# Moving the semaphore reset at the end of a kernel beside its last store

One NeuronCore of one Trainium2 chip runs the kernel. The metric is the device time of one execution in microseconds. The kernel before takes 121.06 us in its first three runs (median).

Some terms. The engines are PE (TensorE), ACT (ScalarE), DVE (VectorE), GpSimd (POOL in the views) and SP (SyncE), which here issues the transfers. A semaphore is a counter that instructions and transfers change and for whose value an engine can wait; each of the big transfers here adds sixteen to its semaphore when it lands, in steps of one. An event-semaphore instruction only waits for and changes semaphores. A drain is another instruction that can carry such waits and changes; the reset drain also names a range of semaphores. A range clear sets a range of semaphores to zero. A barrier is a place in the program that all engines must reach before any goes on.

## The reference

```python
# x, y: (1024, 4096) float32
z = x + y
out = 0.5 * z * (1 + np.tanh(np.sqrt(2 / np.pi) * (z + 0.044715 * z ** 3)))
```

The kernel reads 33.55 MB, writes 16.78 MB and does a few operations per element in between.

## The kernel before

Inputs come in by eight loads of 4 MB, the result goes out by three stores of 8, 5 and 3 MB, all on SP's queue. Eight semaphores count the completions of these eleven transfers; the last store shares its semaphore, number 103, with an early load, so that 32 means that both have landed. Cuts from the kernel, with "..." where lines are left out and two comments added:

```python
    stores = [16384, 10240, 6144]            # columns of float32, 128 partitions
    ...
    def store(i):
        a, b = sr[i]
        ins = nc.sync.dma_start(out=ov[:, a:b], in_=zt[:, a:b])
    ...
    ctx.close()
    tc.close()
    tc.compile()
    begin_early(nc, 2)                       # the first two loads start before the opening barrier
    wait_late(nc)
```

The framework ends a program so: SP waits for everything, all engines meet in a barrier, GpSimd resets and clears the semaphores 99 to 109, all engines meet again. An earlier tuning step had already split this. SP waits for everything but the last store; the barriers run while that store is under way; GpSimd's reset drain, which carries the wait for the last store, and its range clear stand at the very end:

```python
def wait_late(nc):
    body, end = nc.main_func.blocks[1:3]
    SP, POOL = mybir.EngineType.SP, mybir.EngineType.Pool
    last = [i for i in body.instructions if isinstance(i, mybir.InstDMACopy)][-1]
    (sem,) = [u.id for u in last.sync_info.on_update]
    all_done = end.instructions[0]
    clear = next(i for i in end.instructions if isinstance(i, mybir.InstDrain) and i.is_reset_sema)
    assert all_done.engine == SP and clear.engine == POOL and clear.sync_info is None
    waits = all_done.sync_info.on_wait
    its = [w for w in waits if w.id == sem]
    assert len(its) == 1
    rest = [w for w in waits if w.id != sem]

    def drain(old, waits, **reset):
        return mybir.InstDrain(
            name=old.name, engine=old.engine, debug=old.debug,
            sync_info=mybir.SyncInfo(on_wait=waits, on_update=[]), **reset
        )

    at = end.instructions.index(clear)
    clears = [
        drain(
            clear, its, is_reset_sema=True,
            reset_range_start=clear.reset_range_start, reset_range_stop=clear.reset_range_stop,
        ),
        end.instructions[at + 1],
    ]
    assert isinstance(clears[1], mybir.InstISA) and clears[1].engine == POOL
    del end.instructions[at : at + 2]
    end.instructions[0] = drain(all_done, rest, is_reset_sema=False)
    end.instructions.extend(clears)
```

On GpSimd, the end of the program is then, in order:

```
drain                                            first barrier
event semaphore: wait for 4 arrivals, subtract 4
event semaphore: release the 4 others
drain                                            second barrier
event semaphore: wait for 4 arrivals, subtract 4
event semaphore: release the 4 others
drain with reset of 99..109, waits for semaphore 103 >= 32
range clear of 99..109
```

## Time and profile before

| | before |
|---|---|
| time, first three runs | 121.06, 121.23, 121.06 us |
| span of the profiled run, first to last instruction | 118.914 us |
| last store issued | 106.771 us |
| last data packet of it ends | 118.254 us |
| its 16 semaphore increments | 118.329 to 118.689 us |
| reset drain | 118.713 to 118.790 us |
| range clear | 118.819 to 118.914 us |
| GpSimd's step of the runtime's closing barrier | 119.441 us |
| last step of the closing barrier | 120.870 us |

The instants come from the trace's records of instructions, packets and semaphore changes, counted from the start of the span. (The prediction gives 118.259 for the last data packet; that is the end of the last of the 4-byte packets that follow the data and count. Nothing hangs on it.) After the program's last instruction the runtime adds a closing part. In it, semaphore 2 takes nine steps (the first barrier, its last step at 119.726), then some 250 semaphores are written, then it takes nine steps more (120.514 to 120.870); both barriers together are called the closing barrier here. The **tail** is the distance from the sixteenth increment of the last store to the last step of the closing barrier: here 120.870 − 118.689 = 2.181 us. The **own part** is the distance from the same increment to the waiting engine's own step of that barrier: here 119.441 − 118.689 = 0.752 us.

The list of DMA issues on the page gives the last store, with its size and the time from issue to landing:

```profile
out_dram<-z SPq DMA_DIRECT2D x1, 3072.0 KB, 11.9
```

The reader is to see that 11.9 us of store separate its issue from the end.

### The profile page before, as it was taken

The numbers are of one execution on the slowest core, as the hardware profiler recorded it, in microseconds if no ns is written. First come the engines' busy times: TensorE is split into PE (matmuls) and PEld (weight loads), VectorE is DVE, ScalarE is ACT, GpSimd is POOL, SyncE is SP. The second block draws the span as 40 slices with busy tenths as digits, with TensorE's granted clock in tenths as the row PEclk, the third lists the DMA queues.
The fourth block names the chain that finished last, engine by engine and source line by source line (L and its number), as shares of the span: only waits on it lengthen the run. The fifth ranks groups of instructions, "written<-read, shape, count | busy, mean of one in ns | idle before, by whom it ended". The sixth has DMA issues, their size and how long they took to land.

```text
span 118.9 us, 170 instructions
## 1 busy us (share of the span) xinstructions
DVE 73.7 (62%) x35; ACT 61.0 (51%) x34; POOL 69.7 (59%) x19
## 2 busy tenths in 40 slices
DVE  0000000635799995749999958999994999990000
ACT  4000000064888865197698657888829769800000
POOL 0000000699995199999959999959999990000000
DMA  7989898989999898989899998998898889999996
GB/s 254 452 364 518 353 529 353 518 364 474 408 430 452 364 518 353 529 353 518 364 474 408 408 474 353 529 529 353 353 683 375 353 353 441 441 441 441 397 397 265
DMA packets 1584, 50.33 MB, mean 423 GB/s; under 512 B 176, under 2 KB 176, under 8 KB 176
## 3 DMA queue, kind: packets, MB, share of 16 engines
q1 hardware_dynamic: 1584, 50.33, 98.6%
HBM read 33.55 MB, written 16.78 MB: 423 GB/s over the span
## 4 chain that ended last, share of the span: by engine, by line
DMA 51%; POOL 26%; POOLq 4%; DVE 4%; DVEq 2%; ACT 2%; issue 0%; SPq 0%
DMA y<-in_y_dram 51%; POOL z L145 26%; POOLq L223 4%; DVE w L156 2%; DVEq L223 2%; DVE z L168 2%; ACT w L150 2%; SPq L121 0%; POOLq L145 0%
## 5 line engine op out<-in xcount | busy, mean ns | idle before, releaser
L145 POOL TENSOR_TENSOR z<-z,y 128x2048 f32<-128x2048 f32 x15 | 69.4, 4661 | 28.2 <-DMA y<-in_y_dram 28.2
L150 ACT ACTIVATE w<-z 128x2048 f32<-128x2048 f32 x16 | 30.1, 1882 | 37.6 <-DVE z L145 21.4
L156 DVE SCALAR_TENSOR_TENSOR w<-w,z 128x2048 f32<-128x2048 f32 x16 | 36.7, 2295 | 11.2 <-ACT w L150 11.0
L168 DVE TENSOR_TENSOR z<-w,z 128x2048 f32<-128x2048 f32 (+1 forms) x17 | 35.9, 2155 | 0.0
L161 ACT ACTIVATE w<-w 128x2048 f32<-128x2048 f32 x16 | 29.7, 1855 | 4.4 <-DVE w L156 4.3
L145 DVE TENSOR_TENSOR z<-z,y 128x2048 f32<-128x2048 f32 x1 | 2.3, 2292 | 20.4 <-DMA y<-in_y_dram 20.4
L208 ACT ACT_TABLE_LOAD x1 | 1.3, 1283 | 1.3 <-PEq L240 1.3
L207 DVE MEMSET one<- 128x1 f32 x1 | 0.1, 59 | 1.3 <-PEq L240 1.3
L240 POOL MEMSET const-float32-0.0<- 128x1 f32 x1 | 0.1, 99 | 0.2 <-issue 0.2
L208 ACT ACTIVATE one<-one 128x1 f32<-128x1 f32 x1 | 0.2, 203 | 0.0
L240 POOL MEMSET const-bfloat16-1.0<- 128x1 bf16 x1 | 0.1, 101 | 0.0
L240 POOL MEMSET const-uint8-127<- 128x1 uint8 x1 | 0.1, 101 | 0.0
L240 POOL MEMSET const-float32-1.0<- 128x1 f32 x1 | 0.1, 98 | 0.0
## 6 DMA issues: line engine op xcount, KB each, us to landing
z<-in_x_dram SPq DMA_DIRECT2D x4, 4096.0 KB, 31.3
y<-in_y_dram SPq DMA_DIRECT2D x4, 4096.0 KB, 22.2
out_dram<-z SPq DMA_DIRECT2D x1, 5120.0 KB, 15.8
out_dram<-z SPq DMA_DIRECT2D x1, 3072.0 KB, 11.9
out_dram<-z SPq DMA_DIRECT2D x1, 22.0
```

Source lines behind the costliest of these rows:

```text
L145: eng.tensor_add(out=zt[:, a:b], in0=zt[:, a:b], in1=yt[s][:, o : o + b - a])
L150: nc.scalar.activation(out=wt[c], in_=zt[:, a:b], func=act.Square, scale=root)
L156: nc.vector.scalar_tensor_tensor(out=wt[c], in0=wt[c], scalar=c1, in1=zt[:, a:b], op0=alu.add, op1=alu.mult)
L161: nc.scalar.activation(out=wt[c], in_=wt[c], func=act.Sigmoid)
L168: ins = nc.vector.tensor_mul(out=zt[:, a + o : a + o + n], in0=wt[c][:, o : o + n], in1=zt[:, a + o : a + o + n],)
L207: nc.vector.memset(one, 0.0)
L208: nc.scalar.activation(out=one, in_=one, func=act.Sigmoid)
L223: tc.compile()
L240: nc = _bacc.Bacc("TRN2", target_bir_lowering=False, num_devices=1)
```

## The change

The intent is to leave nothing after the landing but a wait. GpSimd resets and clears beside the running store. It must leave out the last store's semaphore, which is still counting, so the range is cleared in two parts around it. At the end an event-semaphore instruction waits for the count and takes it back to zero by subtraction.

```diff
--- before.py
+++ after.py
@@ -26,36 +26,44 @@
 def wait_late(nc):
 
 
-    body, end = nc.main_func.blocks[1:3]
-    SP, POOL = mybir.EngineType.SP, mybir.EngineType.Pool
-    last = [i for i in body.instructions if isinstance(i, mybir.InstDMACopy)][-1]
+
+    body, end = (b.instructions for b in nc.main_func.blocks[1:3])
+    last = [i for i in body if isinstance(i, mybir.InstDMACopy)][-1]
     (sem,) = [u.id for u in last.sync_info.on_update]
-    all_done = end.instructions[0]
-    clear = next(i for i in end.instructions if isinstance(i, mybir.InstDrain) and i.is_reset_sema)
-    assert all_done.engine == SP and clear.engine == POOL and clear.sync_info is None
+    all_done = end[0]
+    reset = next(i for i in end if isinstance(i, mybir.InstDrain) and i.is_reset_sema)
+    at = end.index(reset)
+    clear = end[at + 1]
+    first, stop = reset.reset_range_start, reset.reset_range_stop
+    assert all_done.engine == mybir.EngineType.SP and reset.engine == mybir.EngineType.Pool
+    assert isinstance(clear, mybir.InstISA) and clear.engine == mybir.EngineType.Pool
     waits = all_done.sync_info.on_wait
-    its = [w for w in waits if w.id == sem]
-    assert len(its) == 1
-    rest = [w for w in waits if w.id != sem]
-
-    def drain(old, waits, **reset):
-        return mybir.InstDrain(
-            name=old.name, engine=old.engine, debug=old.debug,
-            sync_info=mybir.SyncInfo(on_wait=waits, on_update=[]), **reset
+    (its,) = [w for w in waits if w.id == sem]
+
+    end[0] = mybir.InstDrain(
+        name=all_done.name, engine=all_done.engine, debug=all_done.debug, is_reset_sema=False,
+        sync_info=mybir.SyncInfo(on_wait=[w for w in waits if w.id != sem], on_update=[]),
+    )
+    parts = []
+    for f, e in ((first, sem), (sem + 1, stop)):
+        if f < e:
+            nc.gpsimd.sem_clear(range(f, e))
+            parts.append(nc.cur_bb.bb.instructions.pop())
+    end[at + 1 : at + 2] = parts
+    end.append(
+        mybir.InstEventSemaphore(
+            name=clear.name, engine=clear.engine, debug=clear.debug,
+            sync_info=mybir.SyncInfo(
+                on_wait=[its],
+                on_update=[
+                    mybir.SyncUpdate(
+                        sync_type="semaphore", id=sem, ant_name=its.ant_name,
+                        update_mode="sem-sub-imm", update_value=its.wait_value,
+                    )
+                ],
+            ),
         )
-
-    at = end.instructions.index(clear)
-    clears = [
-        drain(
-            clear, its, is_reset_sema=True,
-            reset_range_start=clear.reset_range_start, reset_range_stop=clear.reset_range_stop,
-        ),
-        end.instructions[at + 1],
-    ]
-    assert isinstance(clears[1], mybir.InstISA) and clears[1].engine == POOL
-    del end.instructions[at : at + 2]
-    end.instructions[0] = drain(all_done, rest, is_reset_sema=False)
-    end.instructions.extend(clears)
+    )
 
 
 @with_exitstack
```

On GpSimd the end is now:

```
drain, event semaphore, event semaphore          first barrier
drain with reset of 99..109
range clear of 99..102
range clear of 104..109
drain, event semaphore, event semaphore          second barrier
event semaphore: wait for semaphore 103 >= 32, subtract 32
```

## The prediction

> **What bounds the kernel now.** I read the page from the top: span, busy shares, the row of slices, the DMA queue. After that I looked only at the end, because the change touches nothing else.
>
> ```profile
> span 118.9 us, 170 instructions
> DVE 73.7 (62%) x35; ACT 61.0 (51%) x34; POOL 69.7 (59%) x19
> DMA  7989898989999898989899998998898889999996
> q1 hardware_dynamic: 1584, 50.33, 98.6%
> ```
>
> No compute engine is above 62%, while the packets of the one DMA queue fill 98.6% of the span. The kernel is bound by moving 50.33 MB, and the diff leaves every load, add, activation and store as it is. So the first 106 us cannot move by design. Next I listed the DMA queue's own waits and cut the last twelve microseconds into windows.
>
> ```profile
> SPq L223 <- DMA out_dram<-z: 4.2, 1, 4.2
> ...
> 106.70:111.40 4.70, 0.04 (x1) 0.00 (x0) 0.00 (x0) 1.00 0.84 363
> 111.40:118.20 6.80, 0.00 (x0) 0.00 (x0) 0.00 (x0) 1.00 0.94 405
> 118.20:118.72 0.52, 0.00 (x0) 0.00 (x0) 0.00 (x0) 1.00 0.00 0
> 118.72:118.91 0.19, 0.00 (x0) 0.00 (x0) 0.00 (x0) 1.00 0.00 0
> ```
>
> The reader is to see four stages. SP waits 4.2 us for the second store. Until 118.2 the last store moves at about 400 GB/s with no engine at work. For 0.5 us no byte moves, because the store's completion is still on its way. In the last 0.19 us nothing moves and nothing is waited for. Which instructions fill that last piece is told by the line on which the program's end is recorded, first in the window 118 to 119, then in the window 111 to 113:
>
> ```profile
> L223 POOLq DRAIN  x1: 77/77/77, 118.7 to 118.7; - x1
> L223 POOLq EVENT_SEMAPHORE_RANGE_CLEAR  x1: 95/95/95, 118.8 to 118.8; - x1
> ...
> L223 POOLq EVENT_SEMAPHORE  x4: 17/17/17, 111.7 to 112.1; - x4
> L223 POOLq DRAIN  x1: 41/41/41, 111.9 to 111.9; - x1
> ```
>
> The first two lines are the last two instructions of the span: the reset drain, 77 ns, and the range clear, 95 ns. The next two say that GpSimd (POOL) was through the closing barriers at about 112.1 and then sat in the drain's wait for 6.6 us. The chain of waits is of no use here: it counts working instructions and stops with a drain on DVE that began at 104.5, long before the end.
>
> The trace's own records give these instants more finely (from the span's start): the last data packets of the last store end at 118.259; its sixteen semaphore increments are recorded from 118.329 to 118.689; the drain starts at 118.713 and ends at 118.790; the range clear runs from 118.819 to 118.914, where the span ends. The clears of semaphores 99 to 109 are recorded at 118.840 to 118.887.
>
> **What the Trainium skill says.** "Perfetto Trace Analysis", section "Per-instruction lifecycle", sequencer-only instruction: the reported start is the moment when all semaphores are satisfied, and the wait is outside the reported window. The trace agrees: the drain's record begins 24 ns after the sixteenth increment and not at 112. "DMA: Bandwidth & Descriptors", section "Why a DMA increments its semaphore by 16 and not by 1": each engine that took part posts one increment after its own data, and only the full count means that everything landed. The trace agrees, with sixteen records spread over 360 ns; so the wait cannot be taken earlier, it can only be followed by less. "Runtime: NRT & Kernel Launch", section "The ~15µs preamble/postamble breakdown": after the kernel a barrier waits for all engines, then each engine resets 51 semaphores, then another barrier. The trace agrees in kind: the barrier semaphore, number 2, has two steps at 112.45 and 112.49, then none until 119.44, which is 0.53 us after GpSimd's last instruction; resets of 51 semaphores each follow, and the last barrier step is at 120.87.
>
> **The change part by part.**
>
> 1. Removed from the end, between the arrival of the last increment and the end of the span: the drain (77 ns), the gap after it (118.819 − 118.790 = 29 ns) and the range clear (95 ns). Sum 77 + 29 + 95 = 201 ns. All of it is on the path: GpSimd is the only engine still running, and nothing else works in the last window.
>
> 2. Added at the end: one event-semaphore instruction that waits for the last store's count and subtracts it. The same kind is in the barriers on the same engine at 17 ns each (the row x4 above; one of these also waits and subtracts). In the second barrier the last increment is recorded at 112.012, the instruction starts at 112.037, 25 ns later, and its subtraction is recorded at 112.062. So the reaction, 24 ns for the drain and 25 ns for this kind, is the same, and the duration is 17 ns instead of 201.
>
> 3. Moved to the middle: the reset drain and now two clears, one below and one above the last store's semaphore, between the first and the second barrier. Cost there: the drain 77, a gap 29, a clear 95, a gap 29, a clear 95, together 325 ns on GpSimd, holding the second barrier and the other engines up by about as much: its end goes from about 112.2 to about 112.5. The last count comes at 118.689, so 6.2 us of slack stay. Nothing of it is on the path. The two clears write semaphores, no bytes of the store's; I give the DMA nothing for them.
>
> 4. The sum: the span ends at 118.689 + 0.024 + 0.017 = 118.730 instead of 118.914, which is 0.184 us less. The time around the span, 121.08 − 118.91 = 2.17 us in the profiled run, has a closing part that starts only when GpSimd arrives (the barrier semaphore stood still for 7 us), so I carry the saving over one to one: 121.06 − 0.18 = 120.88 us, or 0.15%.
>
> **The rivals.**
>
> First: the saving is hidden, because something else ends then. For it: a tail of 2.17 us lies outside the span and I see only its semaphores. Against: all other engines are through their last instruction by 112.22, and the barrier's third step comes only after GpSimd. If it were so, the time would stay 121.06.
>
> Second: the saving is larger. GpSimd needs 0.53 us from its last instruction to its step of the closing barrier; the first step, at 112.45, comes 0.24 us after the last engine to leave the barrier before it has ended. If part of the surplus of 0.29 us is GpSimd settling after the drain and the clear, it could go too, and the time would be about 120.6 to 120.75. Nothing in the trace says what the 0.53 us are, so I count this only as a longer lower tail.
>
> Third: the new wait costs what the old pair cost. If the subtraction had to be confirmed before the engine goes on, the gain would shrink by some tens of nanoseconds, to 120.93 or so. Against: the same kind in the barrier is 17 ns and its subtraction is recorded 25 ns after its start, within the time that the range clear takes for its own writes (21 to 68 ns after its start).
>
> Fourth: the reset drain, now run while the store is under way and still naming the whole range, wipes the half-full count of the last store's semaphore. The wait would then never be met and the kernel would hang. Against: in the trace of before no semaphore changes during the drain (118.713 to 118.790); the first zeroing is recorded at 118.840, inside the range clear. The drain as such clears nothing that is recorded.
>
> Fifth: the stores run differently by chance. The three runs before span 0.17 us, as much as the expected gain; one slow arrival can hide it in a single run, though hardly in medians of several.
>
> **Range and chances.** Central value 120.88. The lower end, 120.70, is the central value less about 0.18 for the second rival and for scatter; the upper end, 121.05, is the central value and the 0.17 us by which the runs of before differ, which is also nearly no gain at all. Over 2% faster would be below 118.64, a saving of 2.4 us, twelve times what the removed instructions last: 0.005. Over 2% slower would need a new wait of 2.4 us at the end: 0.005. Within 2%: 0.99.
>
> **What would show each step.** In the changed profile the window of the end should hold one event semaphore of about 17 ns on GpSimd in place of the drain and the range clear, starting some 25 ns after the sixteenth increment. Two range clears and a drain of about 77 ns should stand near 112, and the second barrier should be about 0.3 us later there. The distance from the last increment to the span's end should be about 0.04 us instead of 0.225; it is the cleanest number, because it does not contain the store's own scatter. The distance from there to the last barrier step should stay 1.96 us; if it shrinks, the second rival is right; if it grows by 0.18, the first. The prediction fails if the time stays within some hundredths of 121.06 in paired runs although the end is shorter, or if the last store itself lands at another time.

## The result

| | before | changed |
|---|---|---|
| time, median of six runs | 121.09 us (121.03 to 121.23) | 120.94 us (120.86 to 120.96) |
| ratio | | 0.9985, interval 0.9972 to 0.9998 |
| span of the profiled run | 118.914 us | 118.683 us |
| last store issued | 106.771 us | 106.776 us |
| sixteenth increment | 118.689 us | 118.641 us |
| last instruction starts, ends | 118.819, 118.914 us | 118.666, 118.683 us |
| increment to end of span | 0.225 us | 0.042 us |
| own part | 0.752 us | 0.603 us |
| tail | 2.181 us | 2.036 us |

Ratios and intervals are worked out from runs of the same rounds; they are not quite the ratios of the medians quoted. The gain is 0.15%, by the interval between 0.02 and 0.34 us. The page of the changed kernel:

```profile
span 118.7 us, 172 instructions
DMA  7989898989989898989999898998899889999896
q1 hardware_dynamic: 1584, 50.33, 98.8%
```

Same packets, same bytes, the same fill of the queue; two instructions more. The windows of the end in the changed kernel (stretch, its length, busy time of DVE, ACT and POOL with counts, clock, DMA share, GB/s):

```profile
111.40:118.20 6.80, 0.00 (x0) 0.00 (x0) 0.00 (x0) 1.00 0.93 401
118.20:118.67 0.47, 0.00 (x0) 0.00 (x0) 0.00 (x0) 1.00 0.00 0
118.67:118.68 0.01, 0.00 (x0) 0.00 (x0) 0.00 (x0) 1.00 0.00 0
```

The piece after the landing, 0.19 us before, has shrunk to one of 0.01 (two instructions' records to one). The line on which the program's end is recorded is now L231. Its instructions in the window 118 to 119 of the changed kernel (count, shortest, median and longest in ns, first and last start):

```profile
L231 POOLq EVENT_SEMAPHORE  x1: 17/17/17, 118.7 to 118.7; - x1
```

The same line in the window 111 to 113:

```profile
L231 POOLq EVENT_SEMAPHORE  x4: 17/17/17, 111.7 to 112.3; - x4
L231 POOLq DRAIN  x2: 34/58/82, 111.8 to 112.1; - x2
```

And the line of the two clears:

```profile
L50 POOLq EVENT_SEMAPHORE_RANGE_CLEAR  x2: 53/60/66, 112.0 to 112.0; - x2
```

All as the diff says: one event semaphore of 17 ns at the end, both clears and a second drain near 112 us. The drain and the clear that lasted 77 and 95 ns are gone from the end. And yet the tail is not 183 ns shorter, as the span's end is (0.225 − 0.042), but 145 (2.181 − 2.036). The 38 ns between are the one thing to be explained.

**What the measured time contains.** In the trace of before the time of the same execution, 121.08, exceeds the last barrier step, 120.870, by 0.21 us. In the changed kernel it is 120.89 − 120.677 = 0.21. In the twelve traces below it is 0.22 to 0.23 in eleven; the exception is told there. So, where all else is equal, a nanosecond of tail is a nanosecond of time. This matters for the method: the time scatters by tenths of a microsecond, the tail by one to three nanoseconds in the two kernels that were traced twice (the kernel before has one trace).

### The profile page after: what moved, and what is told of

It reads as the page before. It is cut to its first block, busy times and chain, and to the rows that moved or that the text cites. A ratio compares the mean times of both kernels' runs of the same rounds, so it can differ in the third digit from the quotient of the medians.

```text
span 118.7 us, 172 instructions
## 1 busy us (share of the span) xinstructions
DVE 73.7 (62%) x35; ACT 61.0 (51%) x34; POOL 69.6 (59%) x19
## 4 chain that ended last, share of the span: by engine, by line
DMA 51%; POOL 26%; POOLq 4%; DVE 4%; DVEq 2%; ACT 2%; issue 0%; SPq 0%
DMA y<-in_y_dram 51%; POOL z L153 26%; POOLq L231 4%; DVE w L164 2%; DVEq L231 2%; DVE z L176 2%; ACT w L158 2%; SPq L129 0%; POOLq L153 0%
```

## The experiments

Two theories of the 38 ns. **The record**: an instruction at the end costs its recorded duration, and the 38 ns are something else in the runtime's closing part. **The slot**: an instruction costs the time from its start to the next one's start, and part of that lies outside the record. The barrier in the middle of the trace of before shows slots on GpSimd: event semaphore with subtraction 112.037 to 112.115, 78 ns, though recorded as 17; drain at the end 118.713 to 118.819, 106 ns, recorded as 77. A third question is what the remaining half microsecond of GpSimd's own part is. Every run gave the right result. All edits are to `wait_late` of the changed kernel and are shown shortened; `late(name, engine, waits, updates, kind)` builds one instruction with the given waits and semaphore updates, an event semaphore by default. `its` is the wait for 32, `sub` the subtraction of 32; `at_least(n)` and `subtract(n)` stand for the same with another number.

### Eight more instructions at the end, first try

```diff
+    for k in range(8):
+        end.append(late(f"I-9000{k}", POOL, [its], []))
     end.append(late("", POOL, [its], [sub]))
```

> Eight more event-semaphore instructions on GpSimd, each waiting on the last store's count that is already met, stand ahead of the changed kernel's last one. They magnify one disputed number: what such an instruction costs at the end. Theory of the record: it costs its recorded 17 ns, so 8 x 17 = 0.14 us over the changed kernel: about 121.08 us, and the distance from the sixteenth increment of the last store to the last step of the closing barrier (call it the tail; 2.181 us in the kernel before, 2.036 in the changed one) becomes 2.17. Theory of the slot: it costs what lies between the starts of two neighbours on GpSimd, 78 to 79 ns in the barrier of the trace before, so 8 x 78 = 0.62 us: about 121.56 us, tail 2.66. Rival that time at the end is hidden outside the span: the tail may grow, but the time stays 120.94.

Measured: tail 2.390 us; time 121.35 us, ratio to before 1.0022 (1.0008 to 1.0037). The window 118.2 to 121 of this kernel shows why neither number fits:

```profile
L232 POOLq EVENT_SEMAPHORE  x5: 17/43/43, 119.4 to 119.7; - x5
```

Five, not nine: the compiler had packed the waits in pairs (43 ns with two waits, 17 with one). These are four instructions more than in the changed kernel, and they made the tail 2.390 − 2.036 = 0.354 us longer, 88 ns for each on average. As a test of the two theories this run is spoilt. It still answers the first rival: the tail is 0.209 us above that of before, and the time is 0.0022 x 121.1 = 0.27 us above it (0.10 to 0.45). What happens at the end is not hidden.

### Eight more instructions, mended

```diff
+    for k in range(8):     # wait for 32, 31, ... 25, subtract 1 each
+        end.append(late(f"I-9000{k}", POOL, [at_least(32 - k)], [subtract(1)]))
-    end.append(late("", POOL, [its], [sub]))
+    end.append(late("", POOL, [at_least(24)], [subtract(24)]))
```

> The magnifier of the first call again, mended: there the eight waits on one count were packed in pairs, so it did not have eight more instructions. Here each of the eight waits for a smaller count and subtracts one, which cannot be packed; the last one subtracts the remaining 24. Theory of the record: 8 x 17 = 0.14 us more than the changed kernel, tail 2.17. Theory of the slot (78 ns from start to start): 8 x 78 = 0.62 us more, tail 2.66, about 0.48 us over the kernel before. If each subtraction has to come back before the next wait can be met, more than 78 ns each, up to about 100, tail up to 2.85.

Measured: tail 2.800 us, 0.764 more than the changed kernel; time 121.79 us against 120.98 of the changed kernel in the same rounds, ratio to before 1.0057 (1.0044 to 1.0070). The line of the end, window 118.2 to 121:

```profile
L245 POOLq EVENT_SEMAPHORE  x9: 17/17/17, 118.8 to 119.6; - x9
```

Nine instructions, each recorded as 17 ns, yet the first starts at 118.823 and the last at 119.590: 96 ns from start to start. By the records they are busy 0.15 us; they take 0.77. The record theory is out by a factor of five and a half, and the time follows the tail (0.81 us in medians, 0.764 in tails). The slot is 96 and not 78, which is the third case of what was expected, in which each wait here has to see the count that the subtraction just before it has left; the size fits, but that cause was not tried apart.

### Without the subtraction

```diff
-    end.append(late("", POOL, [its], [sub]))
+    end.append(late("", POOL, [its], []))
```

> The changed kernel without the subtraction: its last instruction only waits. (The semaphore is left at 32; the runtime's closing reset takes it to zero.) If the subtraction must be confirmed before GpSimd goes on, as the third rival of the prediction has it, the tail shrinks by some tens of nanoseconds, to 1.97 to 2.01 us. If it is posted and costs nothing, or next to it, the tail stays 2.02 to 2.04. The first run with extra waits hints at a slot of 65 ns for a wait alone against 78 for wait and subtraction: then 2.023.

Measured: tail 2.006 us, 30 ns less than the changed kernel's 2.036; own part 0.573 against 0.603. Time 120.90 us against 120.98, ratio to before 0.9984 (0.9971 to 0.9998). The line of the end, window 118.2 to 121:

```profile
L230 POOLq EVENT_SEMAPHORE  x1: 17/17/17, 118.7 to 118.7; - x1
```

The line of the trace is the same as in the changed kernel, to the nanosecond: 17 ns with the subtraction and 17 without. The 30 ns (27 against the changed kernel's trace of the same rounds) are therefore spent after the recorded end. That is most of the 38 ns that were missing. From the end of the span to the last barrier step, before has 1.956 us, this kernel 1.965 and the changed one 1.994. All six traces in which GpSimd's last instruction subtracts, one of them with a drain, have 1.992 to 1.994 there. The 9 ns that are left between a range clear and a bare wait were not taken apart. (Semaphore 103, left at 32 here, has one more change on record, at 119.861, in the runtime's closing part; all runs were right.)

### Half the change: the drain early, the clear at the end

```diff
-    end[at + 1 : at + 2] = parts
-    end.append(late("", POOL, [its], [sub]))
+    del end[at + 1]
+    end.append(<the range clear of 99..109, now with its wait>)
```

> Half of the change alone: the reset drain goes early, but the whole range is cleared at the end in one instruction, which now carries the wait itself. Taken away from the kernel before: the drain and the gap after it, 77 + 29 = 106 ns. If the end is simply a sum of instructions, the tail is 2.181 - 0.106 = 2.075 us and the time 0.11 below before, about 120.98. If only the drain counted and the clear were free, the tail would be that of the changed kernel, 2.036. If only the clear counted, it stays 2.18.

Measured: tail 2.076 us, where the sum of instructions gave 2.075. The line of the end, window 118.2 to 121:

```profile
L235 POOLq EVENT_SEMAPHORE_RANGE_CLEAR  x1: 95/95/95, 119.2 to 119.2; - x1
```

So the drain was worth 2.181 − 2.076 = 105 ns of the change's 145, and the exchange of the clear for the waiting subtraction only 2.076 − 2.036 = 40. The time, 121.24 us, ratio 1.0007 (0.9988 to 1.0026), can't show this: three of its six runs are at 121.46 to 121.50 and three at 120.88 to 121.01. In the trace, which is of one of the longer three, the last load landed at 80.538 us instead of 80.022, long before anything that was changed. This scatter of half a microsecond in the loads is in other kernels of the same rounds too, and is why the tail decides here.

### A drain in place of the event semaphore

```diff
-    end.append(late("", POOL, [its], [sub]))
+    end.append(late("", POOL, [its], [sub], mybir.InstDrain, is_reset_sema=False))
```

> The changed kernel, with its last instruction replaced by a drain that waits for the same count and subtracts it. Theory of the record: the drain lasts 34 to 82 ns against 17, so the tail is 17 to 65 ns longer than the changed kernel's 2.036: 2.05 to 2.10. Theory of the slot: drain and gap take 63 to 111 ns against 78 for the event semaphore, so the tail is -15 to +33 ns away: 2.02 to 2.07, although the span by the record ends later after the last increment. In time within 0.05 us of the changed kernel, about 120.95.

Measured: tail 2.102 us, 66 ns more than the changed kernel and outside both expectations. Time 121.02 us, ratio 0.9999 (0.9980 to 1.0017). The line of the end, window 118.2 to 121:

```profile
L230 POOLq EVENT_SEMAPHORE  x1: 17/17/17, 118.6 to 118.6; - x1
L230 POOLq DRAIN  x1: 34/34/34, 118.7 to 118.7; - x1
```

The compiler had split it: a waiting event semaphore at 118.615, and 51 ns later the drain with the subtraction. Two instructions, so two slots: 51 ns for the added wait and 34 − 17 = 17 ns for the longer record make 68, against 66 measured. The run does not tell the theories apart as meant, but it puts a number to one more instruction at the end. The slot of a wait without a subtraction is 51 ns here and 65 in the first experiment (119.369 to 119.434), so it depends on what follows.

### Fourteen more clears in the middle

```diff
+    for k in range(7):
+        for f, e in ((first, sem), (sem + 1, stop)):
+            nc.gpsimd.sem_clear(range(f, e))
+            parts.append(nc.cur_bb.bb.instructions.pop())
     end[at + 1 : at + 2] = parts
```

> The changed kernel with fourteen more range clears in the place where two stand, between the two barriers near 112 us. Each takes 79 to 87 ns from start to start there, so GpSimd and the second barrier come about 14 x 0.085 = 1.2 us later, at 113.5 instead of 112.3, with 5 us to spare. If the moved work is hidden as I say, the time stays at the changed kernel's 120.94 and the tail at 2.036. If work on semaphores beside the running store cost anything, say by holding up its increments, the fourteen would make it seven times as large as in the changed kernel: the last increment would come later than 118.7 by more than the few hundredths by which it varies.

Measured: tail 2.034 us, as in the changed kernel within 2 ns. Time 121.02 us, ratio 1.0000 (0.9983 to 1.0017). The line of the added clears in its trace:

```profile
L66 POOLq EVENT_SEMAPHORE_RANGE_CLEAR  x14: 47/56/66, 112.6 to 113.7; - x14
```

And the event semaphores of the two barriers, on the line of the program's end, window 110 to 116:

```profile
L234 POOLq EVENT_SEMAPHORE  x4: 17/17/17, 112.2 to 113.9; - x4
```

The last of the four barrier instructions starts at 113.9 instead of 112.3 (0.49 us of that is the later end of the loads and computing in this trace, the rest the clears), and it changes nothing at the end. One part of the expectation has to be read with care: the sixteenth increment came at 119.160, later than 118.7. But the store was issued at 107.233, 0.457 us later than in the changed kernel, before the first clear ran, and the last load had landed at 80.491 instead of 80.034. From issue to sixteenth increment the store took 11.93 us. In the other kernels it took 11.87 (changed), 11.92 (before) and up to 12.00 (without subtraction). No cost of the clears is to be seen; anything below a tenth of a microsecond would drown in the store's own scatter. The clears end at 113.753 and the first increment comes at 118.782, so clears at the moment of the increments themselves were not tried.

### The wait on another engine

The changed kernel's last instruction, given in turn to SP, DVE, PE and ACT:

```diff
-    end.append(late("", POOL, [its], [sub]))
+    end.append(late("", mybir.EngineType.SP, [its], [sub]))     # or DVE, PE, Activation
```

> The changed kernel, with its last instruction (wait for the last store's count, subtract it) given to SP instead of GpSimd. The question is what the 0.5 us are that GpSimd takes from its last instruction to its step of the closing barrier. Theory: they are GpSimd's own closing instructions, which can run during the store once GpSimd does not wait; then the first barrier steps beside those of PE and ACT come near 112.6 and the tail (sixteenth increment to last barrier step, 2.036 us in the changed kernel) shrinks by 0.2 to 0.5 us, to 1.5 to 1.8; time 0.2 to 0.5 us under the changed kernel, about 120.4 to 120.75. Rival: every engine needs that long after its last instruction, or the barrier's later part is what is long; then the tail is 1.95 to 2.05 and the time 120.9.

> The same with DVE as the engine that waits last. Theory of GpSimd's own closing work: tail 1.6 to 1.9 us, between SP's and the changed kernel's if DVE comes ahead of SP in the barrier. Rival: 1.95 to 2.05.

> The same with the PE as the engine that waits last. In the traces so far the first step of the closing barrier comes 0.29 us after the start of PE's last barrier instruction, and PE is thought to be first in the barrier's order. If so, all other engines follow it: tail = 0.025 + 0.29 + some 0.08 for the two hops until GpSimd's step + the 1.43 that follow GpSimd's step in every trace = 1.82 us. That is 0.2 us less than the changed kernel in spite of being the first in the order, if GpSimd's 0.5 us are its own closing work. Rival: 2.2 us or more, because GpSimd's 0.5 us follow after PE's step.

> The same with ACT as the engine that waits last. Theory of GpSimd's own closing work: about as PE less one hop, 1.75 to 1.85 us. Rival: 2.2 us or more.

| engine that waits last | barrier steps before the landing | own part | tail | time, median of four | ratio to before |
|---|---|---|---|---|---|
| PE | 0 | 0.354 us | 1.859 us | 120.76 us | 0.9965 (0.9942 to 0.9989) |
| ACT | 1 | 0.178 us | 1.783 us | 120.37 us | 0.9947 (0.9914 to 0.9979) |
| GpSimd (the changed kernel) | 2 | 0.603 us | 2.036 us | | |
| DVE | 3 | 0.231 us | 1.619 us | 120.52 us | 0.9944 (0.9925 to 0.9964) |
| SP | 4 | 0.175 us | 1.484 us | 120.40 us | 0.9935 (0.9916 to 0.9954) |

The last instructions in the traces of SP, DVE and PE, on the line of the end, window 118.2 to 121, SP first, then DVE, then PE:

```profile
L230 SPq EVENT_SEMAPHORE  x1: 17/17/17, 118.7 to 118.7; - x1
```

```profile
L230 DVEq EVENT_SEMAPHORE  x1: 21/21/21, 118.7 to 118.7; - x1
```

```profile
L230 PEldq EVENT_SEMAPHORE  x1: 51/51/51, 118.7 to 118.7; - x1
```

One and the same instruction, all starting at 118.7, gives tails from 1.48 to 2.04 us. The column of steps gives the order of the closing barrier: PE, ACT, GpSimd, DVE, SP; an engine can take its step when those ahead of it have. The column of own parts says that GpSimd needs 0.60 us from the landing to its step and SP 0.175. GpSimd's surplus goes when GpSimd does not wait, so it is its own closing work, which runs beside the store. The traces show this work itself: from the start of GpSimd's last instruction to its step pass 0.578 us in the changed kernel (118.666 to 119.244), and 0.578 again where DVE or SP waits last (112.296 to 112.874, 112.309 to 112.887). It is as long as before and lies beside the store. (The expectation for SP had put those steps near 112.6.) SP gains twice: 0.603 − 0.175 = 0.428 us of own part, and (2.036 − 0.603) − (1.484 − 0.175) = 0.124 us in the rest. Of the 0.124, 0.067 are the two steps of DVE and SP that no longer follow GpSimd's; from SP's step on, the first barrier ends after 0.164 us instead of 0.219, and the cause of that was not sought. Together the gain is 0.552. The rivals of these four runs (1.95 us and more, 2.2 and more for PE and ACT) fall. For PE, 1.82 was worked out and 1.859 measured; DVE and ACT came within what was expected; SP came slightly below its 1.5 to 1.8.

ACT is the exception mentioned above: its time is 0.10 us less than its last barrier step instead of 0.22 more, and the last but one step comes 0.17 us after the one before it, where other traces have 0.034. Its own part is as good as SP's, and one of its four runs is at 121.06. Why its time and its tail disagree is open. By time alone, ACT (120.33 to 120.41 us in three runs) cannot be told from SP (120.37 to 120.40), so that a late place in the order pays is shown by the tails, and by the times of PE, DVE and SP only.

### Changed kernel and SP version side by side

> The changed kernel itself once more, so that it stands beside the next three on one chip in the same rounds. Its tail (sixteenth increment to last step of the closing barrier) should again be 2.03 to 2.04 us, and it should be 0.15 us, give or take 0.1, under the kernel before.

> The version in which SP waits last, once more, beside the changed kernel. Tail 1.48 us as in its first run, 0.55 under the changed kernel and 0.70 under the kernel before; the time should show the same differences: about 120.4 us if the kernel before is at 121.1.

| same chip, same rounds | time, median of five | ratio to before | tail |
|---|---|---|---|
| before (nine runs) | 121.07 us (120.96 to 121.31) | | 2.181 us (first trace) |
| changed | 120.98 us (120.87 to 121.26) | 0.9993 (0.9980 to 1.0006) | 2.033 us |
| SP waits last | 120.43 us (120.34 to 120.62) | 0.9947 (0.9935 to 0.9960) | 1.483 us |

The tails repeat to 3 ns. In times the changed kernel is 0.09 us ahead of before in medians here and its interval takes in 1; in the first rounds it was 0.15 with an interval that did not. Both agree with the 0.145 us of the tail. The SP version is 0.55 us ahead of the changed kernel, in the times as in the tails, and beats both kernels: half a per cent under before. It does no less: every store is waited for before the program ends, and every semaphore is back at zero.

## Why the prediction was right

**The time.** 120.88 us was predicted and 120.94 measured, inside 120.70 to 121.05, and within 2% as given 0.99. The size of the gain was predicted as 0.184 us and is 0.145 by the tail. Of the 0.06 us between prediction and measurement, 0.04 is this; the rest is that the kernel before stood at 121.09 in six runs and not at 121.06.

**What bounds the kernel.** Right: bytes, packets and the stages before the landing are the same, and only the end moved. (The last store landed 0.048 us earlier in the changed kernel's trace, 118.641 against 118.689, which the prediction named as a sign of being wrong; it took 11.87 us against 11.92, and 11.86 to 12.00 over all traces, so this is scatter, and the tail leaves it out.)

**Step 1, what is removed.** Right. The 106 ns of drain and gap were tested alone: 105.

**Step 2, what is added.** This is the term of the sum that was mis-sized. The prediction put the event semaphore in with its recorded 17 ns and so said that the distance from the end of the span to the last barrier step "should stay 1.96 us". It is 1.994. The end of the record fell where it was predicted, 0.042 us after the last increment against 0.041. But 30 ns of subtraction follow it unrecorded, as the run without the subtraction shows, and the clear that went had no such part of that size. The trace of before would have told: the same kind on the same engine had its next neighbour 78 ns after its start, against 95 + 29 = 124 for the clear if its gap is like the drain's. The sum of slots, an estimate from these numbers, is 106 + 124 − 78 = 152 ns, near the 145 measured. The Trainium skill would have warned of it, though without a size. "Perfetto Trace Analysis", section "Per-instruction lifecycle", the section that the prediction took the start of a record from, says a few lines on that the propagation of the semaphore update is outside the profile, and calls it the "hidden tail" of every sequencer instruction. The prediction used the one half and not the other.

**Step 3, what is moved.** Right that it is free, shown with sixteen clears in place of two. Its size was too high: between the first barrier's release and the second barrier's wait GpSimd took 445 ns instead of 250, so 195 more and not 325. The two clears are shorter (53 and 66 ns) than the one at the end (95) on which the prediction sized them, and they clear fewer semaphores (four and six against eleven); no run clears the same number in both places, so whether the number or the place makes the difference is not shown. And part of the delay fell into time in which GpSimd had been waiting for the other engines.

**Step 4, one to one.** Right: 0.21 us from the last barrier step to the end of the time, in both kernels and in all traces but ACT's.

**The rivals.** The first, a hidden saving, falls with both runs of extra instructions. The second, that part of GpSimd's 0.53 us belongs to the drain and the clear, falls for the change: the distance grew instead of shrinking. But the suspicion behind it was worth more than the change: the surplus is GpSimd's own, and an engine without it saves 0.43 us. The third, a subtraction that has to be confirmed, came true in the size that was given for it (some tens of nanoseconds, to 120.93); it should have been in the central value. That the engine waits for a confirmation is not shown: the run without the subtraction shows only that about 30 ns go with it. The fourth, a reset drain that wipes the running count, did not come true: every result is right, and of the semaphores 99 to 109 none changes during that drain (111.842 to 111.924; only 96 and 97, those of the barrier under way, do); the clears of 99 to 102 are recorded at 111.975 and later, those of 104 to 109 at 112.050 and later, and 103 counts on. The fifth, scatter, is real: in the second set of rounds the changed kernel cannot be told from before by time alone.

## What to carry to other kernels

In these runs work after the last landing was paid in full, and work beside the last transfer had no cost that could be seen. So at the end of a program keep one instruction, and try it on the engine that reaches the closing barrier soonest and stands last in its order: here SP, which gave 0.55 us where taking two instructions off GpSimd gave 0.15. For instructions that only wait for and change semaphores, take the distance between the starts of neighbours as their cost and not the recorded duration, and take it from a like place: nine that record 17 ns each took 96 each in a chain, 78 in the program's barrier, and a wait alone 51 to 65. When the expected gain is smaller than the scatter of the time, look for a distance in the trace that holds the change and not the scatter, and check once, with a magnified change, that the time follows it.

## What the Trainium skill lacked or had wrong

- "Runtime: NRT & Kernel Launch", section "The ~15µs preamble/postamble breakdown", gives the closing barrier one figure. The runs show that it depends on which engine comes last: from the landing to that engine's step 0.175 us (SP), 0.178 (ACT), 0.231 (DVE), 0.354 (PE) and 0.603 (GpSimd), in the order PE, ACT, GpSimd, DVE, SP. Its 355 ns for eight hops in the opening barrier agree with the last barrier of the changed kernel, 120.677 − 120.320 = 0.357 us.
- "Perfetto Trace Analysis", section "Per-instruction lifecycle", says that the semaphore update is outside the recorded window, and is right, but has no size: on GpSimd about 30 ns for one subtraction, 96 ns from start to start for a chain of waits and subtractions on one semaphore, with 17 ns recorded.
- No page that I found has the range clear: 47 to 53 ns recorded for four semaphores and 66 for six, in a row, 95 for eleven as the last instruction, whose zeroing is on record 21 to 68 ns after its start; nor the drain with a reset on GpSimd: 77 to 83 ns recorded, 106 to 112 from its start to that of the next instruction.
